# Split weights in seven named places, attention steps in another order, the experts' gate loaded behind the second rows

## The chip, the core and the metric

The kernel runs on one core of one Trainium2 chip. The metric is the device time of one execution in microseconds (us). PE is the matrix engine, PEld its weight loads, DVE the vector engine, ACT the scalar engine, POOL the GpSimd engine, SP the engine that here only issues transfers. L404 is line 404 of the kernel before. SBUF is the on-chip memory (tiles below are given per partition); PSUM holds matmul results in 8 banks of 128x512 fp32.

## What is computed (the reference, cut to what matters)

One layer of a diffusion backbone over 512 latent tokens and 256 context tokens, width 1024:

```python
h = ada_rmsnorm(x, g_mix, sh1, sc1); hc = ada_rmsnorm(ctx, ...)
proj = h @ w_in; proj_c = hc @ w_in[:, :CTX_COLS]
o_att = neighbourhood_attention(q, k, v, k_c, v_c, rpb)       # 8 heads of 64
x_l, x_c = short_conv(...), short_conv(...)                   # width 4
h_f, h_b = lru_direction(forward), lru_direction(backward)    # gated linear recurrences
o_lru = (h_f + h_b) * gelu(proj[..., LG])
y = sigmoid(ga) * (o_att @ w_up_attn) + sigmoid(gb) * (o_lru @ w_up_lru)
x = x + ga1 * (y @ w_out)
h2 = ada_rmsnorm(x, g_ffn, sh2, sc2)
x = x + ga2 * hier_moe(h2, ...)   # 32 experts, top 2 in the best group, SwiGLU
return rms(x) * g_final
```

All weights are fp32. The expert weights alone are 32 x 6 MB = 192 MB.

## The kernel before, in words

The order on each engine comes from a planner of the framework: the program is traced in order, and the planner puts each instruction into its engine's queue when its model says that it can run. `tc.high_priority()` moves instructions up, `tc.issue_after(i)` keeps an instruction behind `i` in its engine's queue; `queued()` (L69) does that along the chain `tail[0]`, so that PE's matmuls keep the traced order. A tile that is allocated again waits for the users of the place.

**Splitting weights.** The projections run at nearly fp32 accuracy as three fp32r products (`mm3`, L47: hi x hi, hi x lo, lo x hi). `wsplit` (L52) loads a raw weight tile by SP (L57), copies it to `hi` by ACT (L60, a cast) and subtracts on DVE (L61) to give `lo`. Raw and `lo` share a rotation of 4 places ("wlo"), `hi` has 3 ("whi"); later raw has a pool of its own with 2 places ("wraw"). A place has 4 KB, so it is 7 places and then 9. `next_weights` (L323) hands the weights out in a fixed order and traces the split of the weight after the one handed out.

**Stage 1 (to about 70 us):** modulation, norms, and the value projection `v_add` (L216), whose four weights also go through `wsplit`.

**Stage 2 (to about 465 us):** four rounds j of two heads each. `start` (L628) runs `keys`, `queries`, `lru_x(2j)`, then the first `scores(j, 0)`, then `lru_x(2j+1)`. `proj` (L334) is 8 x 3 matmuls of 512 columns for the latent part, in three pieces with a `yield` after each, and for keys and lru_x 24 of 256 columns for the context. `scores` (L391) writes two PSUM banks ("at"), one per head z; DVE adds the bias and finds the maximum (L411), ACT takes the exponential (L413), DVE the reciprocal (L414), ACT scales (L415): the result is P. `attend` (L421) goes over four blocks b: two steps of other work (`between`), `scores(b+1)`, then for each head four transposes of P into the single bank "pt" (L433), its copy to PT by DVE (head 0) or ACT (head 1) (L436), and one or two steps; then the product with the values (L444) and one step. The steps are `others(j)` (L638): gates, the LRU gates `lru_g` (L486), the LRU outputs `lru_o`, and in between `mod2` (L540), which loads the second part of the modulation weights on POOL's queue (L548) and sums them up on DVE (L552). The PSUM pool has at 2, pt 1, po 1, pj 4 banks. In `lru_g` a single tile "tr" holds the decay's gate of one direction, and the second direction's gate needs it again.

**Stage 3 (to about 530 us), "lift":** `lift` (L592) multiplies with the two up-projections in turn (weights `ua`, 12 matmuls, and `ul`, 24), DVE and ACT combine and split the result.

**Stage 4 (to 612 us):** output projection, router, top-2; POOL scatters token, weight and norm to DRAM tables `std` (L823); the first pair's rows are gathered by matmuls (L837).

**Stage 5 (from 612 us):** 16 pairs of experts. SP streams their weights, 12 transfers of 1 MB a pair ("w<-in_ew", L926), into 24 slots of 8 KB: `w0` to `w8` on the right side of SBUF, twelve `left` slots, and `we0` to `we2`. `wpool` (L888) says in which order they are used. `gu` (L1097) multiplies with the gate and up weights, 4 matmuls a chunk (L1102), `down` (L1107) with the down weights (L1115). For each later pair POOL gathers its token rows by an indirect transfer (`rows`, L950, L952), ACT scales them (L958), PE transposes (L962). `combine` (L1007) multiplies with the routing weight and with `ga2`, the residual's gate (L1012), and PE adds the result to the tokens (L1021, L1022). Before the first `rows`, POOL loads the eight `std` tables (L893), DVE sums them up (L894) and forms the token numbers `toki` (L900). The load of `ga2` (L1135, POOL, 512 KB by broadcast) goes into SBUF that the early slots `we1` and `we2` held, so it waits for the chunk with number 6:

```python
        rows(toki[:, 1:2])
        pgu[0] = [ps4.tile([128, 512], F32, name=f"g{v}") for v in range(2)]
        for pr in range(NE // 2):
            for k in range(1 if pr > 1 else 0, NK):
                if pr == 0 and k == EARLY[1] + 1:
                    wrx.close()
                    ...
                    G.dma_start(ga2, modd[3:4, :].to_broadcast([128, D]))
```

## Time and profile before

| | |
|---|---|
| median of 3 runs | 1086.6 us (1085.23 to 1088.78) |
| profiled execution, own time | 1088.48 us |
| its span, first to last instruction | 1086.7 us |
| mean granted TensorE clock | 0.978 |
| busy PE / DVE / ACT / POOL | 1003.9 / 558.2 / 430.1 / 95.9 us |
| moved by all DMA queues | 294.41 MB, 271 GB/s |

In the rows below, "PE pt L433 <- DVE PT L436: 14.4, 6, 3.7" reads: PE, at the instruction of line 433 that writes pt, waited for what DVE did in line 436, 14.4 us in total, 6 times, 3.7 us at the longest. In a timeline, [3.70 <-DVE PT L436] is the idle time of that engine before the row. A window's row has the busy time of each engine, the number of instructions, the granted clock (1.00 is 2.4 GHz, 0.50 is 1.2 GHz), the share of time in which the 16 DMA engines were busy, and GB/s.

### The profile page before, as it was taken

The numbers are of one execution on the slowest core, as the hardware profiler recorded it, in microseconds if no ns is written. First come the engines' busy times: TensorE is split into PE (matmuls) and PEld (weight loads), VectorE is DVE, ScalarE is ACT, GpSimd is POOL, SyncE is SP. The second block draws the span as 40 slices with busy tenths as digits, with TensorE's granted clock in tenths as the row PEclk, the third lists the DMA queues.
The fourth block names the chain that finished last, engine by engine and source line by source line (L and its number), as shares of the span: only waits on it lengthen the run. The fifth ranks groups of instructions, "written<-read, shape, count | busy, mean of one in ns | idle before, by whom it ended". The sixth has DMA issues, their size and how long they took to land. (4 is left out here: it accounts for less than half of the span.)

```text
span 1086.7 us, 13890 instructions
## 1 busy us (share of the span) xinstructions
PE 1003.9 (92%) x5226; PEld 619.7 (57%) x5226; DVE 558.2 (51%) x1146; ACT 430.1 (40%) x760; POOL 95.9 (9%) x160
## 2 busy tenths in 40 slices
PE   8999999897998998989999959999999999989895
PEld 7787667665776785768887523344444444333332
DVE  5678649576866566746557412333333353312224
ACT  4334873477267749823222112222222222212214
POOL 0021111011110001020100220000000000000001
PEclk9999999899999999999999979999999999999998
DMA  9585235244642222196597978999999999999992
GB/s 371 184 249 169 91 126 196 74 155 131 201 139 73 73 78 88 53 364 208 179 387 274 350 303 348 419 421 420 420 421 420 419 421 420 420 421 421 420 405 108
DMA packets 59176, 294.41 MB, mean 271 GB/s; under 512 B 8720, under 2 KB 9256, under 8 KB 33506
## 3 DMA queue, kind: packets, MB, share of 16 engines
q1 hardware_dynamic: 43634, 252.44, 58.8%
q0 software_dynamic: 12000, 34.75, 9.9%
q10 hardware_dynamic: 3472, 6.30, 1.5%
q8 instruction: 42, 0.69, 0.3%
q14 instruction: 28, 0.23, 0.1%
HBM read 287.76 MB, written 9.65 MB: 274 GB/s over the span
## 5 line engine op out<-in xcount | busy, mean ns | idle before, releaser
L1102 PE MATMUL g<-w,xg 128*64 128x512 f32 x1024 | 232.6, 598 | 5.9 <-DMA w<-in_ew 5.3
L1102 PEld LDWEIGHTS g<-w,xg 128*64 128x64 f32 x1024 | 68.2, 137 | 140.6 <-issue 119.6
L48 PE MATMUL pj<-hh,whi 128*128 128x512 f32 x320 | 132.7, 415 | 4.0 <-ACT gi L499 4.0
L49 PE MATMUL pj<-hl,whi 128*128 128x512 f32 x320 | 128.2, 401 | 0.0
L50 PE MATMUL pj<-hh,wlo 128*128 128x512 f32 x320 | 128.1, 400 | 0.0
L1115 PE MATMUL y<-w,hT 128*64 128x512 f32 x512 | 113.6, 593 | 4.3 <-DMA w<-in_ew 3.7
L965 ACT ACTIVATE xg<-pc,sh2col,s2col 128x128 f32<-128x128 f32 x120 | 45.1, 459 | 156.3 <-PE pc L962 156.3
L995 DVE TENSOR_TENSOR hm<-hm,g 128x512 f32<-128x512 f32 x16 | 11.0, 688 | 179.6 <-PE g L1102 166.4
L1024 DVE TENSOR_TENSOR x<-x,pc 128x512 f32<-128x512 f32 x122 | 75.8, 679 | 14.3 <-PE pc L1022 14.3
L1115 PEld LDWEIGHTS y<-w,hT 128*64 128x64 f32 x512 | 34.9, 137 | 79.4 <-issue 60.0
L61 DVE TENSOR_TENSOR wlo<-wlo,whi 128x1024 fp32r<-128x1024 f32 (+1 forms) x45 | 54.3, 1206 | 47.4 <-ACT whi L60 47.3
L48 PEld LDWEIGHTS pj<-hh,whi 128*128 128x128 f32 x320 | 61.2, 191 | 21.0 <-ACT gi L499 6.5
L1012 DVE SCALAR_TENSOR_TENSOR hm<-y,stok,ga 128x512 f32<-128x512 f32 x31 | 23.3, 751 | 95.4 <-PE y L1115 95.3
L1013 ACT CAST y_h<-hm 128x512 fp32r<-128x512 f32 x31 | 19.2, 619 | 133.3 <-DVE hm L1012 77.0
L50 PEld LDWEIGHTS pj<-hh,wlo 128*128 128x128 f32 x320 | 61.1, 191 | 15.0
L60 ACT CAST whi<-wlo 128x1024 fp32r<-128x1024 f32 (+1 forms) x45 | 46.6, 1035 | 56.5 <-DMA wlo<-in_wcol 37.3
L49 PEld LDWEIGHTS pj<-hl,whi 128*128 128x128 f32 x320 | 61.4, 192 | 12.3
L1021 PE MATMUL pc<-y_h,ot 128*128 128x512 f32 x122 | 52.2, 428 | 0.0
L1022 PE MATMUL pc<-y_l,ot 128*128 128x512 f32 x122 | 48.9, 401 | 0.0
L497 PE MATMUL pj<-xc,ga 128*128 128x256 f32 (+1 forms) x128 | 47.2, 510 | 1.5 <-ACT ga L533 1.3
L952 POOL DMA_INDIRECT xr<-nd,toki x15 | 16.7, 1112 | 347.4 <-PE pc L999 270.9
L552 DVE SCALAR_TENSOR_TENSOR acc<-m,c,acc 128x1024 f32<-128x1024 f32 x28 | 35.8, 1277 | 11.3 <-DMA m<-in_wm 11.3
(382 smaller groups left out, 1697.8 us busy)
## 6 DMA issues: line engine op xcount, KB each, us to landing
w<-in_ew SPq DMA_DIRECT2D x191, 1024.0 KB, 19.8
wlo<-in_wcol SPq DMA_DIRECT2D x40, 512.0 KB, 3.6
m<-in_wm POOLq DMA_DIRECT2D x32, 512.0 KB, 4.3
wm<-in_wm SPq DMA_DIRECT2D x8, 1024.0 KB, 10.1
bias<-in_rpb POOLq DMA_DIRECT2D x32, 128.0 KB, 2.5
gd<-ga ACTq DMA_DIRECT2D x16, 256.0 KB, 2.0
wraw<-in_ul SPq DMA_DIRECT2D x8, 512.0 KB, 3.8
woraw<-in_wout SPq DMA_DIRECT2D x16, 256.0 KB, 12.9
```

The source lines that it names most:

```text
L48: PE.matmul(o, wh, hh, start=start, stop=False)
L49: PE.matmul(o, wh, hl, start=False, stop=False)
L50: return PE.matmul(o, wl, hh, start=False, stop=stop)
L60: S.copy(hi[:, :n], raw[:, :n])
L61: V.tensor_tensor(lo[:, :n], raw[:, :n], hi[:, :n].bitcast(F32), op=ALU.subtract)
L497: m = PE.matmul(pg[:, 0:n], lw[:, 128 * w:128 * w + 128], xc[:, s0:s0 + n], start=True, stop=True)
L965: S.activation(xg[z][:, k % 4, :], pg[:, k % 4, :], AF.Identity, bias=sh2col[:, k:k + 1], scale=s2col[:, k:k + 1])
L1021: PE.matmul(pc, ot[:, i, :], y_h, start=True, stop=False)
L1022: m = PE.matmul(pc, ot[:, i, :], y_l, start=False, stop=True)
L1024: V.tensor_add(x2[:, i, ns], x2[:, i, ns], pc)
L1102: m = PE.matmul(pgu[pr][v][64 * e:64 * e + 64, :], xg[pr][k // 4][:, k % 4, 64 * e:64 * e + 64], w[:, v, e, :], start=(k == 0), stop=(k == ...
L1115: m = PE.matmul(py[64 * e:64 * e + 64, :], hT[:, k, 64 * e:64 * e + 64], w[:, k % 2, e, :], start=(k == 0), stop=(k == 3))
```

## The change

- `wsplit` takes its three places from `wplaces`: seven named tiles of 4 KB. The first four weights have written-out places; from then on raw rotates over three (2, 0, 1), `hi` over two (3, 5), `lo` over two (4, 6). The pool "wraw" is gone.
- `attend`: the transposes of both heads come first, into the shared "at" banks (now 3; "pt" is gone), then two steps, `scores(b+1)`, one step, the value product, one step. P has 2 places instead of 3.
- `lru_g`: the second direction's decay gate goes into half of `w2`; the decay of the first direction (ACT exponential, tanh, square, two DVE instructions) is traced after the second direction's first gate.
- `mod2_g`: two loading places, and places of their own for its two small tiles; two more yields.
- `start`: the first `scores` come after the latent part of `lru_x(2j+1)`.
- `wout` has two raw places instead of one (one more 2 KB), the unused "gap" pool grows from 18 to 24 KB, and the order of the left slots is adapted: three of them (9 to 11) lie in the gap, where two did before.
- the load of `ga2` is kept behind the first `rows` in POOL's queue.

```diff
--- before.py
+++ after.py
@@ -49,20 +49,30 @@
+    def wplaces():
+
+
+        yield from ((0, 1, 4), (3, 2, 5), (0, 3, 6), (0, 1, 4))
+        n = 0
+        while True:
+            yield (2, 0, 1)[n % 3], (3, 5)[n % 2], (4, 6)[n % 2]
+            n += 1
+
+    wplace = wplaces()
+
     def wsplit(src, shape):
-
         n = shape[0] * shape[1]
-        raw = (wraw[0] or ws).tile([128, 1024], F32, name="wraw" if wraw[0] else "wlo", bufs=2 if wraw[0] else 4)
+        r, h, l = next(wplace)
+        raw = ws.tile([128, 1024], F32, name=f"ws{r}")
         SP.dma_start(raw[:, :n], src)
-        lo = ws.tile([128, 1024], F32R, name="wlo", bufs=4)
-        hi = ws.tile([128, 1024], F32R, name="whi", bufs=3)
+        hi = ws.tile([128, 1024], F32R, name=f"ws{h}")
+        lo = ws.tile([128, 1024], F32R, name=f"ws{l}")
         S.copy(hi[:, :n], raw[:, :n])
...
-    wraw = [None]
     tail = [None]
@@ -391,7 +401,7 @@
         w0 = WIN[b]
-        scs = [ps.tile([128, 512], F32, name="at", bufs=2) for z in range(2)]
+        scs = [ps.tile([128, 512], F32, name="at", bufs=3) for z in range(2)]
         q = slice(128 * b, 128 * b + 128)
@@ -405,7 +415,7 @@
                 sc = scs[z]
-                P = p1.tile([128, 512], F32, name="P", bufs=3)
+                P = p1.tile([128, 512], F32, name="P", bufs=2)
                 st = p1.tile([128, 8], F32, name="st", bufs=4)
@@ -423,18 +433,19 @@
             between(2)
-            ahead_ = scores(j, b + 1, **kq) if b < 3 else None
             pts = []
-            for z in range(2):
-                with tc.high_priority():
-                    pt = ps.tile([128, 4, 128], F32, name="pt")
+            with tc.high_priority():
+                for z in range(2):
+                    pt = ps.tile([128, 512], F32, name="at", bufs=3).rearrange("p (k t) -> p k t", k=4)
                     with queued():
...
                     (S.copy if z else V.tensor_copy)(pts[z], pt)
-                between(1 + z)
+            between(2)
+            ahead_ = scores(j, b + 1, **kq) if b < 3 else None
+            between(1)
             with tc.high_priority():
@@ -484,26 +495,34 @@
         w2 = lp.tile([128, 2, 771], F32, name="w2")
-        for d in range(2):
-            cc = slice(8 * d + c, 8 * d + c + 1)
-            tr = lp.tile([128, 771], F32, name="tr")
-            for g, t in ((0, tr), (1, gi[:, d, :])):
-                w = 2 * d + g
-                bcol = (hba, hbx)[g][:, cc]
-                V.memset(t[:, 256:259], 0.0)
-                for (s0, n) in ((259, T), (0, TC)):
-                    pg = ps.tile([128, 512], F32, name="pj", bufs=4)
-                    with queued():
-                        m = PE.matmul(pg[:, 0:n], lw[:, 128 * w:128 * w + 128], xc[:, s0:s0 + n], start=True, stop=True)
-                    tail[0] = m.ins
-                    S.activation(t[:, s0:s0 + n], pg[:, 0:n], AF.Tanh, bias=bcol, scale=0.5)
-                if w < 3:
-                    yield
-            S.activation(a[:, d, :], tr, AF.Exp, bias=nsp4[:, cc], scale=nsp4[:, cc])
-            S.activation(tr, tr, AF.Tanh, bias=sp4[:, cc], scale=sp4[:, cc])
-            S.activation(w2[:, d, :], a[:, d, :], AF.Square)
-            V.scalar_tensor_tensor(w2[:, d, :], w2[:, d, :], 1.0, tr, op0=ALU.add, op1=ALU.mult)
+        cc = [slice(8 * d + c, 8 * d + c + 1) for d in range(2)]
+        tr = [lp.tile([128, 771], F32, name="tr"), w2[:, 1, :]]
+
+        def decay(d):
+
+            S.activation(a[:, d, :], tr[d], AF.Exp, bias=nsp4[:, cc[d]], scale=nsp4[:, cc[d]])
+            S.activation(tr[d], tr[d], AF.Tanh, bias=sp4[:, cc[d]], scale=sp4[:, cc[d]])
+            sq = lp.tile([128, 771], F32, name="tr") if d else w2[:, 0, :]
+            S.activation(sq, a[:, d, :], AF.Square)
+            V.scalar_tensor_tensor(w2[:, d, :], sq, 1.0, tr[d], op0=ALU.add, op1=ALU.mult)
             V.scalar_tensor_tensor(gi[:, d, :], gi[:, d, :], 1.0, xc, op0=ALU.add, op1=ALU.mult)
+
+        for w in range(4):
+            d, g = w // 2, w % 2
+            t = gi[:, d, :] if g else tr[d]
+            bcol = (hba, hbx)[g][:, cc[d]]
+            V.memset(t[:, 256:259], 0.0)
+            for (s0, n) in ((259, T), (0, TC)):
+                pg = ps.tile([128, 512], F32, name="pj", bufs=4)
+                with queued():
+                    m = PE.matmul(pg[:, 0:n], lw[:, 128 * w:128 * w + 128], xc[:, s0:s0 + n], start=True, stop=True)
+                tail[0] = m.ins
+                S.activation(t[:, s0:s0 + n], pg[:, 0:n], AF.Tanh, bias=bcol, scale=0.5)
+            if w == 2:
+                decay(0)
+            if w < 3:
+                yield
+        decay(1)
         S.activation(w2, w2, AF.Sqrt, scale=0.0625)
@@ -544,22 +563,22 @@
         for k in range(NK):
-            raw = m2.tile([128, 1024], F32, name="m2", bufs=2)
+            raw = m2.tile([128, 1024], F32, name=f"m{k % 2}")
             G.dma_start(raw, A["wm2"][g, k])
...
                 V.scalar_tensor_tensor(acc, raw, c32[:, k, 0:1], acc, op0=ALU.mult, op1=ALU.add)
-            if k < NK - 1:
-                yield
+            yield
         pm = ps.tile([128, 256], F32, name="pj", bufs=4)
...
             PE.matmul(pm[32 * j:32 * j + 32, :], ones[:, 0:32], acc[:, 256 * j:256 * j + 256], start=True, stop=True)
-        mr = m2.tile([128, 256], F32, name="m2", bufs=2)
-        mb = m2.tile([128, 256], F32, name="m2", bufs=2)
+        mr = m2.tile([128, 256], F32, name="mr")
+        mb = m2.tile([128, 256], F32, name="mb")
         V.memset(mb, 0.0)
...
         V.tensor_add(mr, pm, mb)
+        yield
         if g in (0, 3):
@@ -631,8 +650,11 @@
         run(lru_x(2 * j))
+        second = lru_x(2 * j + 1)
+        for _ in range(3):
+            next(second)
         Ps = scores(j, 0, **kq)
-        run(lru_x(2 * j + 1))
+        run(second)
         return kq, Ps
@@ -675,7 +697,6 @@
     yl = [yp.tile([128, NK, 128], F32R, name=f"yl{i}") for i in range(4)]
-    wraw[0] = l2.enter_context(pool("wraw"))
     tas = [lift(A["ua"][m], 4, 0, m) for m in range(2)]
@@ -691,7 +712,7 @@
             G.dma_start(wo["g", nh], modd[0:1, 512 * nh:512 * nh + 512].to_broadcast([128, 512]))
-        raw = pl.tile([128, 512], F32, name="woraw", bufs=bufs)
+        raw = pl.tile([128, 512], F32, name=f"woraw{k % bufs}")
         SP.dma_start(raw, A["wout"][nh, k])
@@ -701,7 +722,7 @@
             for k in (2 * m - 8, 2 * m - 7):
-                wout(0, k, wop, 1)
+                wout(0, k, wop, 2)
         ta = tas[m]
@@ -755,7 +776,7 @@
-    l2.enter_context(pool("gap")).tile([128, 18 * 256], F32, name="gap")
+    l2.enter_context(pool("gap")).tile([128, 24 * 256], F32, name="gap")
     with pool("p3") as p3, ExitStack() as xtx:
@@ -885,7 +906,7 @@
         left = [wx.enter_context(pool(f"w{i}")) for i in range(WR, WR + WL)]
-        wpool += [left[4], *left[10:12], left[0], left[2], *left[5:10], left[1], left[3]]
+        wpool += [*left[9:12], left[0], left[2], *left[4:9], left[1], left[3]]
         slot = chunks()
@@ -949,7 +970,7 @@
-            G.indirect_dma_start(xr, None, nd[:, :], bass.IndirectOffsetOnAxis(ap=tok, axis=0), bounds_check=T - 1,
+            return G.indirect_dma_start(xr, None, nd[:, :], bass.IndirectOffsetOnAxis(ap=tok, axis=0), bounds_check=T - 1,
                                  oob_is_err=False)
@@ -1123,7 +1144,7 @@
         pgu, dw = {}, [None]
-        rows(toki[:, 1:2])
+        rows1 = rows(toki[:, 1:2])
         pgu[0] = [ps4.tile([128, 512], F32, name=f"g{v}") for v in range(2)]
@@ -1132,7 +1153,8 @@
                     ga2 = p6.tile([128, D], F32, name="ga2")
-                    G.dma_start(ga2, modd[3:4, :].to_broadcast([128, D]))
+                    with tc.issue_after(rows1.ins):
+                        G.dma_start(ga2, modd[3:4, :].to_broadcast([128, D]))
                 gu(pr, k)
```

## Rows read from the trace of the kernel before

**Rows 1.** Busy time by windows: PE, PEld, DVE, ACT, POOL, clock, DMA share, GB/s.

```profile
80.00:460.00 380.00, 346.33 (x1881) 263.67 (x1881) 261.73 (x402) 246.00 (x376) 38.86 (x72) 0.98 0.37 119
644.00:658.00 14.00, 9.65 (x36) 5.61 (x38) 3.35 (x5) 5.82 (x11) 1.02 (x1) 0.65 0.26 77
658.00:1054.00 396.00, 387.05 (x1780) 153.26 (x1776) 128.62 (x220) 89.49 (x183) 14.75 (x14) 1.00 1.01 420
```

**Rows 2.** Waits of PE, 80 to 460 us: total us, times, longest us.

```profile
PE pt L433 <- DVE PT L436: 14.4, 6, 3.7
PE at L404 <- ACT qr L356: 6.7, 3, 5.1
PE pj L48 <- ACT gi L499: 4.0, 4, 1.6
PE pj L569 <- DVE m L562: 2.4, 1, 2.4
PE at L404 <- DVE qr L357: 2.1, 3, 0.8
PE pt L433 <- DVE st L414: 1.8, 3, 1.1
```

**Rows 3.** Timeline around block 2 of round 1, on PE, DVE and ACT.

```profile
240.68 0.66 PE L433 MATMUL pt<-ident,P 128*128 128x128 f32 x4
246.39 0.68 DVE L436 COPY PT<-pt 128x512 f32<-128x512 f32 x1
247.13 0.67 PE L433 MATMUL pt<-ident,P 128*128 128x128 f32 x4 [3.70 <-DVE PT L436]
247.18 1.34 ACT L415 ACTIVATE P<-P,st 128x512 f32<-128x512 f32 x2 [1.57 <-DVE st L414]
```

**Rows 4.** Timeline of PE behind the first scores of round 1.

```profile
195.97 0.63 PE L49 MATMUL pj<-hl,whi 128*128 128x512 f32 x1
196.40 0.63 PE L50 MATMUL pj<-hh,wlo 128*128 128x512 f32 x1
200.77 0.39 PE L50 MATMUL pj<-hh,wlo 128*128 128x512 f32 x1
201.01 0.40 PE L48 MATMUL pj<-hh,whi 128*128 128x512 f32 x1
```

**Rows 5.** Splits: idle before whi and wlo (us, times); a cast, a subtraction.

```profile
  DMA wlo<-in_wcol: 25.7, 11
232.25 1.05 ACT L60 CAST whi<-wlo 128x1024 fp32r<-128x1024 f32 x1
235.60 1.22 DVE L61 TENSOR_TENSOR wlo<-wlo,whi 128x1024 fp32r<-128x1024 f32 x1
```

**Rows 6.** Waits of PE, 460 to 660 us.

```profile
PE pj L50 <- DVE wlo L61: 3.1, 2, 1.7
PE pj L48 <- ACT whi L60: 2.1, 1, 2.1
```

**Rows 7.** Timeline at the start of stage 5, on POOL, DVE and PE.

```profile
612.83 1.17 POOL L893 DMA_DIRECT2D s<-std  x2
625.32 0.56 POOL L1135 DMA_DIRECT2D ga<-modd  x1 [10.37 <-issue]
625.86 3.20 POOL L893 DMA_DIRECT2D s<-std  x6
638.71 0.79 DVE L894 TENSOR_REDUCE stok<-s 128x48 f32<-128x384 f32 x1 [11.53 <-DMA s<-std]
629.51 7.09 PE L1115 MATMUL y<-w,hT 128*64 128x512 f32 x32 [0.67 <-ACT hT L1003]
642.23 1.06 POOL L952 DMA_INDIRECT xr<-nd,toki  x1 [13.17 <-DVE y_l L1014]
648.35 1.97 PE L962 MATMUL pc<-ident,xr 128*128 128x128 f32 x8 [11.76 <-ACT xr L958]
653.66 10.58 PE L1102 MATMUL g<-w,xg 128*64 128x512 f32 x48
```

## The prediction, made before the changed kernel ran

> **What bounds the kernel now.** I read the busy times by windows first [rows 1]. From 658 to 1054 us the DMA engines are busy all the time at 420 GB/s: the experts' weights arrive as fast as they ever do here. PE works 387.05 of these 396 us, on chunks that lie ready in 24 slots, and idles only where it has used them up. So the end is the end of the weight stream, plus 33 us of tail. Two things can move it: the moment at which stage 5 begins, which PE sets in stages 1 to 4 (346.33 busy of 380 us in stage 2), and holes in the stream once it runs. One hole is plain: from 644 to 658 us the DMA share is 0.26, so 14 x 0.74 = 10.4 us are lost, with all slots full and PE not consuming. A us taken from PE's idle time before 612 us, or from this hole, is a us at the end. Next I read PE's waits in stage 2 [rows 2], then the rows around single waits [rows 3, 4], the splitting of weights [rows 5], the lift [rows 6] and the start of stage 5 [rows 7].
>
> **a. Shared banks and the new order in attend.** PE's transposes waited 14.4 us in 6 waits for head 0's copy out of the only "pt" bank, and 1.8 us more that end with a DVE row of the same place [rows 2]. In [rows 3] head 0 is transposed at 240.68, DVE copies at 246.39, and head 1 has to wait until 247.13. With three banks head 1 needs no copy first. The copy must now be done when scores(b+1) wants the third bank, two steps later: a step is a third of a latent projection, 24 matmuls at 0.24 us [rows 4] = 5.8 us, so 1.9 us, and two are 3.9. The copy was 5.7 us behind, but with the bias work of scores ahead of it on DVE; that now stands behind it. What is late next is P. In [rows 3] the scores end where the transposes begin, at 240.68, and ACT's last scaling ends at 247.18 + 1.34 = 248.52: 7.8 us. Before, the order left some six steps and more for that; now four steps and the value product, about 7.7 + 1 us, so in an ordinary block 0.9 us is to spare, and in a block whose steps are the short ones of lru_g less. For block 0 there is only the context half of lru_x (256 of 512 columns, 2.9 us) and two steps, 6.8 us: 1 us late, four times. Bounds: 16.2 us gained, and 0 if P takes over everything. I take 10: 16.2 less 4 x 1.0 and 2.2 for the other twelve.
>
> The page TensorE: Matmul & The Clock Gate of the Trainium skill (section on HAM oscillation) speaks against this part: it tells of a kernel whose matmuls were put in a better order and says that "Adding PSUM double-buffering gave no further gain". By that this term is 0 and the sum below 19 instead of 29. The row of 14.4 us stands against it here.
>
> **b. First scores later.** PE waited 6.7 + 2.1 = 8.8 us for the rotated queries, once 5.1 us [rows 2]. Now 5.8 us of projection come first, more than the longest single wait. That work needs its own split weights in time: ACT stood 25.7 us in 11 waits for raw tiles [rows 5]. Three raw places let that load go out one weight earlier. Bounds 0 and 8.8; I take 6, nearer to the whole, since both halves of the cause are touched.
>
> **c. lru_g.** ACT, DVE and PE do the same number of instructions. The second direction's gate no longer waits for "tr", so its banks come free earlier; the wait for them is 4.0 us in 4 [rows 2]. The last gate's banks come free no earlier, as the first decay is now ahead of it on ACT. Bounds 0 to 4; taken 2.
>
> **d. mod2.** PE waited once, 2.4 us, for a small DVE sum that hangs on a load just issued [rows 2]. A yield now stands between. 8 more steps in all fit into the spare `next` calls. Taken 2 of 2.4. The loads themselves stay 32, on the same queue.
>
> **e. Clock.** After a long idle time PE runs at 1.2 GHz: matmuls start 0.43 us apart at 195.97, and 0.24 at 200.77 [rows 4]. In stage 2 the granted clock is 0.98 on average [rows 1], so 380 x 0.02 = 7.6 us are lost. If the waits halve, about half of the slow stretches go: 3.5. Bounds 0 and 7.6.
>
> **f. Seven places.** They add no instruction. Two prices. At the seam to stage 2 the first projection's `lo` takes the place of the value projection's last `lo`, so DVE can subtract only when PE is done with it: one subtraction, 1.2 us, partly behind two matmuls: +1. From then on `hi` and `lo` are two deep, where `hi` had three and `lo` shared four: the cast of weight n+2 cannot begin before PE has left weight n, and has the time of weight n+1. The rows show a cast at 232.25 whose subtraction, begun at 235.60, ends at 236.82 [rows 5]: 4.6 us with the queues' waits, against 5.8 us for a latent-only weight (4 queries, 16 gates, 8 lru_o: 28). It fits by 1.2 us. Bounds: 0, and 28 x 2 = 56 if the queues make 7.8 us of it, as they do for P. I take +4: four are late by 1 us.
>
> **g. Lift.** PE waited 3.1 + 2.1 us for split weights there [rows 6]. The raw pool of the lift lies where stage 2's tiles were; raw tiles in stage 2's own places can be loaded earlier. Against it: `ul` after `ua` has only 12 x 0.24 = 2.9 us for its split (cast 1.05, subtraction 1.2 at least), seven times, and one more early expert chunk (three gap slots, not two) shares the DMA. Bounds: 5.2 gained; 7 x (4.6 - 2.9) = 12 lost. Taken: 3 gained. The wout change and the other slot order cost nothing: DMA-bound stretches take the same bytes.
>
> **h. The gate behind the rows.** POOL issued the load of ga2 at 625.32, when its place came free, and only then six of the eight `std` loads, 625.86 to 629.06; they landed at 638.71, 9.65 us after the last. Then toki, the rows at 642.23, their scaling, and PE, idle for 11.76 us, transposed at 648.35, 6.1 us after the rows' issue [rows 7]. Freed of that, POOL issues the six loads from about 615 (after two of them at 612.83 and the memset) to 618.2; they land at 627.8; 3.5 us of sums and the queue later the rows go out, at 631.3. With 6.1 us to the transposes as before, or 4.7 more if the rows land as slowly as the tables did, PE can transpose from 637.4 to 642.1. It ends pair 0 at 629.51 + 7.09 = 636.6. The gate now goes out at 632.4 and lands at 642; combine waits for it: two steps on DVE and ACT, and PE adds from 643.5. Pair 1's first chunk is multiplied 1.9 to 3.7 us later (eight matmuls at either pace), 645.4 to 647.2 instead of 653.66 [rows 7]; the hole ends as much earlier [rows 1]. So 6.5 to 8.3 us of the hole close; I take 7.5. Bounds 0, if the gate lands as late as before, and the whole 10.4. The new wait is the one for ga2; behind it on POOL only the next pair's rows stand, which are needed in the middle of pair 1.
>
> **Sum.** 10 + 6 + 2 + 2 + 3.5 - 1 - 4 + 3 + 7.5 = 29 us. The profiled execution took 1088.48 us, with a span of 1086.7; less 29 it is 1059.5. It lies 1.9 us above the median of 1086.6, so the median to expect is 1057.6, rounded 1057.5.
>
> **Rivals.** 1. The waits only change their name: DVE and ACT are the late ones, P takes the place of the bank, and what PE gains at the scores it loses at the first transposes. For it: 7.8 us for P against 6.8 and 8.7 of cover. Against it: DVE is busy 261.73 and ACT 246.00 of 380 us [rows 1], neither is full. Then a, b, c and e give nothing: 1057.5 + 21.5 = 1079. What the Trainium skill says under a speaks for this rival, for term a alone. Half-way cases lie between. Chance 0.18.
>
> 2. Slower: the two-deep places. ACT's casts stand in one queue with everything else; if the cast and subtraction need 7.8 us from PE's release on average, each of the 28 latent-only weights makes PE wait 2 us: 56 instead of 4, so 1057.5 + 52 = 1109.5. It decides from 5.8 + 33/28 = 7.0 us on; below that the change is still faster. For it: ACT's casts already come late, 25.7 us of its idle time stand before them [rows 5]. Against it: that was for raw loads, which three places bring earlier, and the cast in the rows took 4.6. Chance 0.11.
>
> 3. All of the waits go, and the hole too: 16.2 + 8.8 + 4 + 2.4 + 7.6 + 5.2 + 10.4 = 54.6 less f's 1: 1033. A good part of that way, 1041, has a chance of 0.06.
>
> 4. The ordering of ga2 does nothing, since the `std` scatters land later than I think and the loads wait for those: h is 0, 1065. It is inside the forecast's own range.
>
> **How the numbers follow.** The forecast with its own range of 1043 to 1070 has 0.60; rival 1 0.18, rival 3 0.06, rival 2 0.11, and 0.05 that gains and losses of f and a cancel to within 0.3% (3.3 us, about what a measurement of this kernel can tell from no change). Faster by over 0.3%: 0.84. The range for 8 in 10 goes from 1041 to 1079: it takes in rival 1's time and most of rival 3's way, and leaves out rival 2, the tie and the far end.
>
> **What would show it.** PE's wait at the transposes for the copy should be gone and a wait for P of some us there instead (a); the wait at L404 for the queries under 3 us (b); waits of PE for whi and wlo in stage 2 of a few us, not tens (f); POOL's six `std` loads done by 620 us less what stage 2 gained, and PE's idle time before the first transposed rows short, followed by one for the gate (h); the DMA hole after pair 0 about 3 us; the stream then unbroken to its end. I am wrong if PE waits for split weights at every gate, or if stage 5 begins at 600 us or later.

## The result: 1056.2 us, and the profile after

The changed kernel takes 1056.17 us (median of 4 runs, 1054.95 to 1057.06), the kernel before 1087.69 in the same comparison: a ratio of 0.9703 [0.9664, 0.9742], or 31.5 us less. The forecast was 1057.5. The sum was right to 1.3 us; most of its terms were not, as the experiments show.

Against [rows 1] the windows of the changed kernel read (busy us of PE, PEld, DVE, ACT, POOL, then clock, DMA share and GB/s):

```profile
80.00:460.00 380.00, 365.27 (x1982) 280.78 (x1981) 274.42 (x418) 250.23 (x384) 43.80 (x83) 0.99 0.42 144
618.00:634.00 16.00, 15.36 (x62) 6.41 (x64) 4.89 (x7) 5.19 (x12) 0.00 (x0) 0.85 0.76 299
634.00:1022.00 388.00, 379.04 (x1744) 150.66 (x1741) 128.64 (x220) 89.26 (x183) 14.69 (x14) 1.00 1.01 420
```

The last stage is what it was: 420 GB/s, PE waiting only for chunks. The hole ahead of it has shrunk from 14 x 0.74 = 10.4 us to 16 x 0.24 = 3.8 us. From 80 to 460 us PE is busy 19 us more of the 380 (in the changed kernel this stretch holds stage 2 and the first 19 us of the lift). Stage 5 begins at 588.15 us instead of 612.43, 24.3 us earlier; the other 7.1 of the 31.4 by which the span shrank lie behind that.

The waits of PE in the same stretch as [rows 2] (total us, times, longest):

```profile
PE pj L48 <- ACT ws L71: 4.2, 1, 4.2
PE pj L48 <- ACT w L520: 3.3, 3, 1.1
PE pj L518 <- ACT gi L520: 3.0, 4, 1.5
PE pj L518 <- ACT tr L520: 1.6, 1, 1.6
PE pj L48 <- ACT gi L520: 1.1, 1, 1.1
PE pj L588 <- DVE mr L580: 0.8, 1, 0.8
PE pj L575 <- ACT w L520: 0.5, 1, 0.5
PE at L442 <- ACT P L425: 0.2, 1, 0.2
```

The wait for head 0's copy (14.4 us) is gone, and that for the rotated queries (8.8) too. P, which I had feared, costs 0.2. But the waits for banks that ACT empties at the gates (L520) are now 9.5 us in these rows where they were 4.8 (4.0 of them in [rows 2]), and the lift waits 4.2 us at once.

The start of stage 5 on POOL, DVE and PE, against [rows 7]:

```profile
590.56 3.23 POOL L914 DMA_DIRECT2D s<-std  x6
602.21 0.69 DVE L1016 TENSOR_TENSOR hm<-hm,g 128x512 f32<-128x512 f32 x1 [13.22 <-ACT hm L1015]
602.81 0.81 DVE L915 TENSOR_REDUCE stok<-s 128x48 f32<-128x384 f32 x1
605.81 1.06 POOL L973 DMA_INDIRECT xr<-nd,toki  x1 [12.03 <-DMA w<-in_ew]
606.88 0.57 POOL L1157 DMA_DIRECT2D ga<-modd  x1
617.18 0.75 DVE L1033 SCALAR_TENSOR_TENSOR hm<-y,stok,ga 128x512 f32<-128x512 f32 x1 [12.26 <-DMA ga<-modd]
614.13 1.10 PE L983 MATMUL pc<-ident,xr 128*128 128x128 f32 x8 [1.82 <-ACT xr L979]
618.64 0.79 PE L1042 MATMUL pc<-y_h,ot 128*128 128x512 f32 x1 [3.41 <-ACT y_h L1034]
622.65 10.52 PE L1123 MATMUL g<-w,xg 128*64 128x512 f32 x48
```

The six table loads no longer stand behind the gate; the last of them lands at 599.4. DVE sums them up only from 602.81 on, as a step of pair 0 that waits for ACT stands ahead in its queue. The token numbers are ready at 604.92, and the rows go out 0.9 us later, as in the kernel before (where the profile names DVE as the releaser). Counted from the start of stage 5, pair 1's first chunk is multiplied after 34.5 us instead of 41.2. The new wait is the one foretold: 3.4 us of PE for the product with the gate.

### The profile page after: what moved, and what is told of

Read it like the earlier page. It is cut to its first block, busy times and chain, and to the rows that moved or that the text cites. A ratio compares the mean times of both kernels' runs of the same rounds, so it can differ in the third digit from the quotient of the medians.

```text
span 1055.3 us, 13907 instructions
## 1 busy us (share of the span) xinstructions
PE 1000.6 (95%) x5226; PEld 618.2 (59%) x5226; DVE 561.5 (53%) x1146; ACT 428.1 (41%) x760; POOL 95.4 (9%) x160
## 4 chain that ended last, share of the span: by engine, by line
PE 75%; DMA 12%; ACT 7%; DVE 4%; issue 1%; ACTq 0%; SPq 0%; DVEq 0%; POOLq 0%
PE g L1123 17%; PE pj L48 10%; PE pj L49 9%; PE pj L50 9%; DMA w<-in_ew 9%; PE y L1136 8%; PE pc L1042 3%; PE pc L1043 2%; DMA ws<-in_ul 2%; PE po L798 1%; PE po L800 1%; PE po L799 1%; PE at L442 1%; PE pv L234 1%; PE pc L983 1%
## 5 line engine op out<-in xcount | busy, mean ns | idle before, releaser
L48 PE MATMUL pj<-hh,ws 128*128 128x512 f32 x320 | 129.7, 405 | 4.4 <-ACT w L520 3.3
L50 PE MATMUL pj<-hh,ws 128*128 128x512 f32 x320 | 126.4, 395 | 1.6 <-DVE ws L72 1.6
L49 PE MATMUL pj<-hl,ws 128*128 128x512 f32 x320 | 126.5, 395 | 0.0
L71 ACT CAST ws<-ws 128x1024 fp32r<-128x1024 f32 (+1 forms) x60 | 59.3, 989 | 73.9 <-PE pj L49 52.5
L72 DVE TENSOR_TENSOR ws<-ws,ws 128x1024 fp32r<-128x1024 f32 (+1 forms) x60 | 69.0, 1150 | 32.6 <-ACT ws L71 32.4
L48 PEld LDWEIGHTS pj<-hh,ws 128*128 128x128 f32 x320 | 60.1, 188 | 21.1 <-ACT w L520 5.3
L50 PEld LDWEIGHTS pj<-hh,ws 128*128 128x128 f32 x320 | 60.0, 188 | 16.6 <-DVE ws L72 2.0
L49 PEld LDWEIGHTS pj<-hl,ws 128*128 128x128 f32 x320 | 60.2, 188 | 12.4
L1042 PEld LDWEIGHTS pc<-y_h,ot 128*128 128x128 f32 x122 | 23.4, 192 | 32.7 <-issue 21.9
```

The lines of the kernel that those rows point to most:

```text
L48: PE.matmul(o, wh, hh, start=start, stop=False)
L49: PE.matmul(o, wh, hl, start=False, stop=False)
L50: return PE.matmul(o, wl, hh, start=False, stop=stop)
L71: S.copy(hi[:, :n], raw[:, :n])
L72: V.tensor_tensor(lo[:, :n], raw[:, :n], hi[:, :n].bitcast(F32), op=ALU.subtract)
L1042: PE.matmul(pc, ot[:, i, :], y_h, start=True, stop=False)
```

## The experiments

Twelve kernels. All medians, ratios and four marks of each profiled execution stand here first, so that a kernel can be looked up: the first matmul of the lift (the end of stage 2), of the output projection, of stage 5, and the span. "f", "d" and so on are the parts of the prediction.

| kernel | median us | ratio to before | lift | out. proj. | stage 5 | span |
|---|---|---|---|---|---|---|
| before | 1087.69 | | 466.6 | 539.9 | 612.4 | 1086.7 |
| after | 1056.17 | 0.9703 [0.9664, 0.9742] | 441.0 | 515.6 | 588.1 | 1055.3 |
| u_attend (after without a) | 1048.91 | 0.9662 [0.9638, 0.9686] | 438.6 | 510.3 | 581.2 | 1046.4 |
| u_scores (without b) | 1056.40 | 0.9719 [0.9693, 0.9744] | 440.5 | 517.7 | 588.3 | 1054.6 |
| u_lru (without c) | 1055.29 | 0.9710 [0.9685, 0.9735] | 439.6 | 516.5 | 589.0 | 1056.5 |
| u_gate (without h) | 1063.80 | 0.9794 [0.9771, 0.9818] | 440.0 | 516.3 | 587.1 | 1060.9 |
| u_places (without f) | 1059.30 | 0.9735 [0.9699, 0.9771] | 451.9 | 522.0 | 592.7 | 1061.6 |
| o_places (before with f) | 1082.37 | 0.9961 [0.9937, 0.9984] | 455.4 | 532.6 | 603.7 | 1078.6 |
| u_abc (before with f, d, h) | 1060.96 | 0.9788 [0.9765, 0.9811] | 445.0 | 522.0 | 592.9 | 1059.0 |
| u_ab (before with f, d, c, h) | 1048.88 | 0.9671 [0.9642, 0.9700] | 447.6 | 513.2 | 583.6 | 1047.5 |
| u_ac (before with f, d, b, h) | 1051.94 | 0.9690 [0.9670, 0.9711] | 436.8 | 514.9 | 585.7 | 1050.2 |
| pair | 1061.45 | 0.9762 [0.9728, 0.9796] | 444.0 | 522.1 | 594.7 | 1058.3 |
| late_chunks | 1056.18 | 0.9719 [0.9685, 0.9754] | 440.6 | 519.0 | 589.9 | 1053.9 |
| best2 | 1046.65 | 0.9631 [0.9613, 0.9650] | 438.7 | 510.0 | 580.7 | 1045.1 |

After, u_gate and late_chunks do the same work on PE up to the lift and reach it at 440.0 to 441.0, so there a mark is good to about 1 us. Each mark is that of a single execution: the profiled one of u_places is the slowest of its six, 4.0 us above their median, and that of u_lru 3.0 above, so their marks may be late.

### One part undone

**Attend** (u_attend):

```
-  scs: "at", bufs=3; P bufs=2; pt shares "at"; transposes, between(2), scores(b + 1), between(1)
+  scs: "at", bufs=2; P bufs=3; pt its own bank; scores(b + 1), transposes with between(1 + z)
-  mr, mb: places of their own
+  mr, mb in m0, m1 (so that the third P fits)
```

> The changed kernel with attend and scores as before: a bank of its own for the transposes, two score banks, three P places, scores(b+1) ahead of the transposes (so that it fits, two small tiles of mod2 share the places m0 and m1). Theory (part a is worth its waits and part of the clock): PE waits again for head 0's copy by DVE, about 16 us in stage 2, and the granted clock there falls from 1.00 to 0.98-0.99, so 4 to 8 us more: 1056 + 20 to 24 = 1076 to 1080 us, stage 5 begins 20 to 24 us later than at 588. Rival (the banks alone give nothing, the waits only move to another name): 1056 to 1060 us, stage 5 begins at 588 to 592 and the wait at the transposes is there, but another wait of the changed kernel is gone.

Measured: 1048.91 us, 7.3 **less**; its six runs (1047.78 to 1052.16) and the changed kernel's four do not overlap. Both the theory and its rival fell: the part costs time. (The edit also takes back the small tiles' own places, which was not tried by itself.) Undone, its old waits are back, but smaller than in [rows 2]:

```profile
PE pt L443 <- DVE PT L446: 7.4, 5, 2.3
PE pt L443 <- DVE st L424: 2.2, 2, 1.1
PE pj L517 <- ACT gi L519: 0.4, 2, 0.2
```

and the waits for gate banks are nearly gone. They are 9 us and more in every kernel with the new attend and 5 or less in every one without it, so in the changed kernel they are what attend's new order made of the old wait. It also slows the scores themselves. On PE's timeline, the twelve matmuls of one block in the changed kernel (the last line is the work behind them):

```profile
214.12 0.73 PE L414 MATMUL at<-kr,qr 64*128 64x256 f32 x4
214.58 0.28 PE L414 MATMUL at<-kx,qp 64*128 64x256 f32 x1
214.69 0.28 PE L414 MATMUL at<-kr,qr 64*128 64x256 f32 x1
214.70 0.28 PE L414 MATMUL at<-kx,qp 64*128 64x256 f32 x1
214.81 0.28 PE L414 MATMUL at<-kr,qr 64*128 64x256 f32 x1
214.82 0.62 PE L414 MATMUL at<-kx,qp 64*128 64x256 f32 x4
215.37 0.50 PE L48 MATMUL pj<-hh,ws 128*128 128x512 f32 x1
```

and with attend undone:

```profile
208.26 0.62 PE L414 MATMUL at<-kr,qr 64*128 64x256 f32 x6
208.72 0.52 PE L414 MATMUL at<-kx,qp 64*128 64x256 f32 x6
209.16 0.33 PE L443 MATMUL pt<-ident,P 128*128 128x128 f32 x1
```

1.25 us against 0.90. Eleven of the sixteen blocks take 1.25 us, one takes 1.13 and four 0.90; the 1.03 that the expectation of "pair" names below is in none. In the program the two heads alternate, one on the lower and one on the upper 64 rows of the array, and in the blocks of 0.90 us the twelve matmuls start two by two. In the block above three start alone, six two by two and three alone, as when one head is three matmuls ahead of the other. I take the reason to be that with three banks in one rotation head 1's bank comes free later than head 0's, so that the planner puts head 0's matmuls first; the order of the queue itself is not in the trace.

The scores lose 4.1 us by it (11 x 0.35 + 0.23). Against that, PE's waits in stage 2 are 1.8 us shorter with the new attend (10.5 against 12.3), and the clock gives 1.7. So without the slower scores the part would gain 3.5 us there; with them the sum is a loss of 0.6, where the mark says 2.3. The other 5 us of the 7.3 lie behind it, 3.0 of them in the lift (74.7 us against 71.7), and have no cause shown.

**First scores, lru_g and the gate, one at a time** (u_scores, u_lru, u_gate):

```
-  three steps of lru_x(2j+1), scores, the rest          (u_scores: scores ahead of lru_x(2j+1))
-  decay(0) behind the third gate, decay(1) at the end   (u_lru: each decay behind its two gates)
-  with tc.issue_after(rows1.ins): load of ga2           (u_gate: load of ga2 unordered)
```

> The changed kernel with the first scores ahead of the second lru_x, as before. Theory (part b): PE waits again for the rotated queries, 7 to 9 us over the four heads' starts, and 1 to 3 us of clock behind the longest of them: 1064 to 1068 us. Rival (the three raw places have already removed the cause, as the late split was what made the queries late): under 2 us of waits at the first scores, 1056 to 1058 us.

> The changed kernel with lru_g as before (one tr place, each direction's decay right behind its two gates). Theory (my sign for part c was wrong: with the first decay put between the third and the fourth gate's Tanh, the banks of these come free later): the 9.5 us of PE's waits for gate banks fall to about 4, the time to 1050 to 1052 us. Rival 1 (the rearrangement is needed, the wait for tr comes back on top): 9 to 14 us of waits, 1056 to 1062 us. Rival 2 (ACT is the engine that is behind here whatever the order): the waits stay within 2 us, 1054 to 1058 us.

> The changed kernel with the load of ga2 not ordered behind the second rows. Theory (part h): POOL holds six of the eight table loads behind ga2's place again, the rows and the first chunk of pair 1 come 7 us later, the DMA hole after pair 0 grows by 7 us: 1062 to 1065 us, stage 5 beginning at 588 as in the changed kernel. Rival (with the front shorter and the slots in another order the place of ga2 is free in time): below 1 us, 1055 to 1058 us.

Measured: 1056.40, 1055.29 and 1063.80. Undoing the first scores brings no wait for the queries back, as its rival said. Undoing lru_g leaves 9.0 us of gate-bank waits (4.5 + 3.3 + 1.2), so rival 2 held and, beside the new attend, lru_g's order was not their cause. The gate is worth 7.6 us, and POOL shows how:

```profile
600.04 0.56 POOL L1156 DMA_DIRECT2D ga<-modd  x1 [10.38 <-issue]
600.58 3.19 POOL L914 DMA_DIRECT2D s<-std  x6
616.33 1.06 POOL L973 DMA_INDIRECT xr<-nd,toki  x1 [12.55 <-DVE y_l L1035]
```

The second rows go out 29.2 us after stage 5 begins, as before (29.8), where the changed kernel has 17.7.

**The places** (u_places) and **the places alone** (o_places):

```
-  r, h, l = next(wplace); raw, hi, lo in ws0 ... ws6
+  raw and lo from one ring of four, hi from a ring of three; the lift's raw pool; gap 18; slots as before
   (o_places: the kernel before with the first of these and not the second)
```

> The changed kernel with the split weights in the places of before (raw and lo in one ring of four, hi in a ring of three, the lift's own raw pool, the gap and slot order of before). Theory (the seven places carry the front gain, since undoing the first scores and lru_g changed nothing and undoing attend made it faster): the waits for the rotated queries come back through late splits, the clock falls below 1.00, 1056 + 14 to 24 = 1070 to 1080 us. Rival 1 (the forecast's term, the places cost 4 + 1 and give 3 at the lift): 1052 to 1058 us. Rival 2 (each part alone is enough to hide the same waits): 1056 to 1060 us.

> The kernel before with the seven places alone (and the gap, the slot order and the output weights' two names that go with them); attend, first scores, lru_g, mod2 and the gate as before. Theory (the places carry the front gain): 1087 - 14 to 22 = 1065 to 1073 us, the waits for the queries, 8.8 us, under 2, stage 2's clock 0.99 or more, ACT's idle time for raw tiles gone. Rival (the places only help with the other parts): 1080 to 1088 us.

Undone, 1059.30; alone, 1082.37: both near the rivals, small effects on the time (alone 4.8 us below 1087.15, the runs of before beside them, a ratio of 0.9961 [0.9937, 0.9984]; undone 3.1 us, with runs that overlap those of the changed kernel). The marks say more. At the end of stage 2 the places are worth 11.2 us alone (466.6 to 455.4) and up to 10.9 when taken from the changed kernel (451.9 against 441.0, from the slowest run of u_places); the lift hands 4 of it back, 73.3 us long before, 77.2 with the places alone. What they do in stage 2 is in ACT's waits from 68 to 440 us. The changed kernel without them:

```profile
ACT whi L60 <- DMA wlo<-in_wcol: 46.6, 17, 4.9
```

The places alone in the kernel before:

```profile
ACT ws L71 <- DMA ws<-in_wcol: 4.1, 1, 4.1
```

The changed kernel, where no such row is left and the casts wait for PE to leave a place:

```profile
ACT ws L71 <- PE pj L49: 34.6, 24, 3.1
```

A cast that waits for its raw load holds ACT, and the subtraction behind it holds DVE. That had also made some of the copies late. The timeline of ACT and DVE in the kernel before, ahead of the copy at 141.60, with PE idle for 2.12 us behind it:

```profile
137.52 1.05 ACT L60 CAST whi<-wlo 128x1024 fp32r<-128x1024 f32 x1 [2.26 <-DMA wlo<-in_wcol]
138.60 1.23 DVE L61 TENSOR_TENSOR wlo<-wlo,whi 128x1024 fp32r<-128x1024 f32 x1 [2.20 <-ACT whi L60]
```

The copy stands behind both, and so does that of 350.33 (a wait of 2.14); with the places alone these two waits are gone. In the block of [rows 3] the same chain held DVE for 0.37 us only: the subtraction, the bias work of scores, a sum of mod2 and a gate fill the 5.1 us from the transposes to the copy, and with the places alone 2.76 of its 3.70 us stay. The copy of 262.39 (a wait of 2.95) was late for another reason, a load of mod2, on DVE:

```profile
259.44 1.28 DVE L552 SCALAR_TENSOR_TENSOR acc<-m,c,acc 128x1024 f32<-128x1024 f32 x1 [4.52 <-DMA m<-in_wm]
```

With the places alone, the two rows of waits at the transposes come to 6.3 us instead of 16.2, the bank being the same. And the casts' new wait costs PE nothing in stage 2: the two-deep price that I had set at 4 did not come.

### Scores in turn, and the lift's loads

**pair**: the twelve score matmuls of a block chained to each other.

```
+  with tc.issue_after(m.ins) if m else nullcontext():
       m = PE.matmul(scs[z][:, cs], ...)
```

> The changed kernel with the twelve score matmuls of a block chained to each other, so that both heads' stay in turn; nothing else. In the changed kernel's queue twelve of the sixteen blocks have head 0's six ahead of head 1's six, and such a block takes 1.03 to 1.25 us from its first start to the next work's start, where the kernel with attend undone takes 0.90. Theory (matmuls on the two halves of the array overlap only when they stand in turn): 12 x 0.13 to 0.35 us, 2 to 4 us less, 1052 to 1054 us, scores' busy time (both rows together) from 26 to 18 us. Rival (the bank for head 1 comes free late, so the group as a whole starts later and PE waits there instead): 1056 to 1060 us, a wait of PE for PT at the scores.

Each block is back at 0.90 us (214.38 to 215.28), and the kernel is 5.3 us slower: stage 2 ends 3 us later, the gate-bank waits go to

```profile
PE pj L520 <- ACT gi L522: 7.8, 8, 2.8
```

and the clock to 0.98 from 180 to 360 us. Neither range was met (1061.45 us is above the rival's 1060), and PE does not wait for PT at the scores, as the rival had it; why the gate-bank waits grow instead was not traced further. So the pace is real, but mending it alone does not pay.

**late_chunks**: the four early expert chunks behind one of the lift's raw loads.

```
-  with tc.issue_after(loaded[0]) if n in late[4:] else nullcontext():
+  with tc.issue_after(loaded[0]) if n in late[4:] else tc.issue_after(raws[-7]):
```

> The changed kernel with the four expert chunks that go out at 435 to 441 us ordered behind the lift's fourth latent weight on SP. Theory (their 4 MB delay the lift's raw weights by some 9 us, DMA share 1.02 in 440:460): the lift's waits, 6.0 us, fall under 2 and the clock from 0.88 to near 1.00 there, 1056 - 5 to 8 = 1048 to 1051 us. Rival (the chunks then delay the later raw weights or the output weights instead, or the wait is ACT's own queue): 1054 to 1058 us.

Nothing (1056.18). The chunks had stood ahead of the lift's weights; on SP, in the changed kernel:

```profile
435.76 2.41 SPq L947 DMA_DIRECT2D w<-in_ew  x3
438.35 0.82 SPq L716 DMA_DIRECT2D woraw<-in_wout  x2
439.55 0.33 SPq L68 DMA_DIRECT2D ws<-in_ua  x1
```

with the cast of that ua at 455.56, 16 us after the issue. But with the chunks gone the output weights moved into their place, and their casts into ACT's queue ahead of the lift's. On ACT and PE in late_chunks:

```profile
449.64 0.62 ACT L719 CAST wo<-woraw 128x512 fp32r<-128x512 f32 x1 [4.30 <-DMA woraw<-in_wout]
451.26 0.79 PE L48 MATMUL pj<-hch,ws 128*128 128x512 f32 x1 [5.08 <-ACT ws L72]
```

### Two and three parts undone: what took the front's time

Attend undone, and with it the first scores (u_ab), lru_g (u_ac), or both (u_abc); the edits are those above.

> The changed kernel with attend and the first scores as before. Theory (with the raw places and mod2's own steps the queries are in time whatever the order; undoing the first scores alone changed nothing): within 2 us of attend undone alone, 1047 to 1051 us, no wait at the first scores. Rival (attend's new order had been hiding the queries' wait, so b and a covered for each other): 6 to 9 us of waits for the queries and some clock, 1055 to 1061 us.

> The changed kernel with attend and lru_g as before. Theory (the gate-bank waits of the changed kernel, 9.5 us, are the price of attend's new order and not of lru_g; with attend undone 1.7 us are left whichever lru_g): 1048 to 1051 us. Rival (lru_g's new order is what removed them, 4 us of waits and the clock behind them come back): 1053 to 1058 us.

> The changed kernel with attend, first scores and lru_g all as before: what is left of the change is the seven places, mod2's two added yields and the gate behind the rows. Theory (undoing the first scores or lru_g beside attend cost 0 and 3 us, so mod2's yields and the places hold the front gain together): 1049 to 1054 us, waits for queries and gate banks under 6 us in all. Rival (the first scores and lru_g's order can each stand in for the other, both out brings their waits of 6.5 and 4.3 us and some 7 us of clock back): 1060 to 1070 us; the places alone had 1082.4, and the gate is worth 7.6, so 1074.8 would mean that mod2's yields give nothing.

Measured 1048.88, 1051.94 and 1060.96. The first two stay near attend undone alone by their times, but u_ab's end of stage 2 is 9.0 us later (447.6 against 438.6), with the waits for the queries back at 5.2 us, as its rival said; the lift hid that, with no wait of PE and 65.6 us. u_ac lies between its theory and its rival, and u_abc met the rival's range. It is 23.7 us below its own runs of before (1084.67); the places alone had 4.8 and the gate has 7.6, so 11.3 are left for mod2's yields, much more than the 2 I gave them. The transposes of mod2 on the timeline, without the yields (o_places):

```profile
261.93 0.44 PE L579 MATMUL pj<-ident,m 128*128 128x128 f32 x2 [3.12 <-DVE m L572]
```

and the window there:

```profile
260.00:270.00 10.00, 8.07 (x32) 6.57 (x33) 7.40 (x11) 1.97 (x3) 1.61 (x3) 0.83 0.55 191
```

With them (u_abc):

```profile
243.35 0.44 PE L579 MATMUL pj<-ident,m 128*128 128x128 f32 x2 [0.29 <-ACT gi L509]
```

Without the yield the sum stands behind lru_g's scans on DVE and PE idles 3.1 us, and the granted clock is 0.83 in the 10 us around that. The clock also falls behind waits of other kinds in o_places (2.8 us for the copy, 2.6 and 2.1 for the queries, and once 1.0), so that it is 0.94 from 180 to 270 and 0.96 from 270 to 360 us (9.0 us); u_abc has 0.98 and 1.00 (1.8 us). How much of the 10.4 us at the mark is the yields' own and how much is waits that fall better by chance stays open: the wait itself is one of 3.1 us. (In u_abc the small tiles lie in the two loading places, as before, so they are not the cause.)

### A faster kernel

**best2**: attend undone, and three edits: the seam's places swapped, the gate behind the last table load, and the chunks and output weights behind the lift's raw loads.

```
-  yield (2, 0, 1)[n % 3], (3, 5)[n % 2], (4, 6)[n % 2]
+  yield (2, 0, 1)[n % 3], (5, 3)[n % 2], (6, 4)[n % 2]
-  with tc.issue_after(rows1.ins): load of ga2
+  with tc.issue_after(tab8.ins): load of ga2
+  with tc.issue_after(raws[-1]) if nh == 0 else nullcontext(): load of woraw
+  the expert chunks as in late_chunks
```

> The kernel with attend undone (1048.9 us) and three edits: the seam's places swapped (hi in places 5 and 3, lo in 6 and 4, so the first projection's lo does not take the value projection's last), the gate of the combination behind the last table load rather than behind the second rows, and at the lift the four early expert chunks and the output weights' first loads ordered behind the lift's raw loads. Theory: the seam's wait of 1.6 us goes, the hole after pair 0 closes by up to 3.9, the lift's waits of 3.2 + 0.5 and the lost clock there (0.07 x 20 + 0.01 x 40 us) go: 1049 - 7 to 11 = 1038 to 1042 us. Rival at the lift (moving the chunks alone changed nothing; the DMA engines were then held by 2 MB of x and the output weights, and ACT's casts stood behind these): no gain there, 1042 to 1045 us. Rival at the gate (the rows now stand behind the gate on POOL and come as much later): hole as before, 3.9 us more than the theory.

Measured 1046.65 us, ratio 0.9631 [0.9613, 0.9650]: the lowest median here, 2.3 us below attend undone, where I had expected 7 to 11 less; the intervals of the two ratios overlap. The seam keeps 1.4 of 1.6 us. The gate closes nothing of the hole: PE's wait of 2.8 us for the gated product becomes one of 2.5 for the rows. At the lift the theory held for as long as nothing stood ahead: PE is busy 20.00 of 20 us from 440 to 460 (16.27 with attend undone alone). Then, on SP,

```profile
460.89 1.95 SPq L948 DMA_DIRECT2D w<-in_ew  x4
462.94 1.17 SPq L69 DMA_DIRECT2D ws<-in_ul  x1
```

and on ACT and PE

```profile
478.62 1.04 ACT L72 CAST ws<-ws 128x1024 fp32r<-128x1024 f32 x1 [2.02 <-DMA ws<-in_ul]
479.72 0.50 PE L48 MATMUL pj<-hch,ws 128*128 128x512 f32 x1 [2.79 <-ACT ws L72]
```

the next raw weight comes 15.7 us after its issue, behind 4 MB. Ordering the chunks behind the last raw weight was not tried.

## Why the prediction was right, and which of its steps were wrong

The sum of 29 was met by 31.4 because wrong terms cancelled, which is luck; h alone came as priced. For stage 2 the terms can be read off the table by adding the parts one by one to the kernel before, at the mark of the lift: f takes 466.6 to 455.4, d to 445.0 (u_abc), b to 436.8 (u_ac), c back up to 438.6 (u_attend), a to 441.0 (after). Each step is one execution against one other, and another order would give other steps.

- **a, forecast +10: wrong in sign.** It costs 2.3 us in stage 2, and 7.3 in all by the medians. The failed step is "the copy was 5.7 us behind" as a price of the bank: the copy was behind late splits, a late load of mod2 and other work of DVE, and f alone, with the bank as it was, removed 9.9 of the 16.2 us. What I had as rival 1 happened to this part, not with P but with gate banks and with heads out of turn. The section on HAM oscillation of TensorE: Matmul & The Clock Gate in the Trainium skill, which I had set aside, said that double-buffering gave nothing further there; here the part with the third bank did not pay either, though the 14.4 us of waits were real. Without b, a does gain in stage 2 (447.6 to 440.5): the two hide the same waits, and I had added them. By the medians it loses there too (1048.88 to 1056.40), for the lift grows by 11.6 us.
- **b, forecast +6:** 8.2 to 9.0 in stage 2 with attend as before, nothing beside the new attend. By the medians it is 9.0 (u_abc to u_ac) and nothing (u_ab to u_attend).
- **c, forecast +2: wrong in sign in stage 2,** where it loses 1.3 to 2.7 us in each of the three pairs (u_lru, u_ac, and u_ab against u_abc). The wait that I priced does go: with attend as before, the gate banks cost 4.9 us without c (u_ac) and 0.7 with it (u_attend). What I left out is that another wait comes in its place. In u_ac, to be set against the rows of u_attend above:

```profile
PE pj L48 <- ACT gi L509: 2.7, 3, 1.5
PE pt L443 <- DVE PT L446: 2.6, 3, 1.3
```

  The wait for the copy is 2.6 us there and 7.4 with c (1.9 and 6.5 in the other pair); why DVE's copy is later was not traced. By the medians c does not lose: 0.9 us, within the noise, beside the new attend, and a gain of 3.0 and 12.1 us with attend as before, where the lift is 6.4 and 11.4 us shorter with it.
- **d, forecast +2:** 10.4 with the clock, the largest miss in size.
- **e, forecast +3.5:** stage 2's clock went from 0.98 to 1.00 between 80 and 440 us, nearly all of the 7.6. It does not come with f: with the places alone the clock is still 0.98 there; in the steps above it is inside d and b.
- **f, forecast -5 (seam 1, two-deep 4): wrong in sign,** +11.2 in stage 2. The seam cost 1.6. The two-deep price of 4 measured 0 in stage 2: the casts wait 34.6 us for PE to leave a place, and PE never waits for a cast. The term left out what the new places give, the end of ACT's waits for raw loads; rows 5 showed them (25.7 us), and I used them only for b. By the medians f gives less, 4.8 us alone and 3.1 in the changed kernel.
- **g, forecast +3: wrong in sign.** From the first lift matmul to the output projection it takes 74.7 us against 73.3, and 65.6 to 78.5 over all kernels with these places (70.2 in u_places). The failed step is that the raw tiles come earlier: a raw weight behind the chunks is ready only 16 us after its issue. I had named one more early chunk and not priced it; but late_chunks, with all four moved, still takes 78.5, so that the chunk is the cause is not shown. The other failed step is that the second raw place of the output weights, part of the same edit, was put at nothing: in the changed kernel ACT's cast of an output weight waits 6.85 us for its load (until 451.57), ahead of the lift's cast at 455.56 that PE waits for. How much of the lift's length is owed to which stays open.
- **h, forecast +7.5:** 7.6 by the medians, and nearly step by step as worked out: rows 17.7 us after stage 5 began (18.9 forecast), transposes 26.0 (25.0 to 29.7), pair 1 at 34.5 (33.0 to 34.8). Two misses inside cancelled: the tables landed after 11.3 us instead of 15.4, and DVE's queue then held their sum for 3.4.

## What to carry to other kernels

When several waits on one engine are to go, price the cause they share before the symptoms: here a late load held an in-order cast, which held an in-order subtraction, which held a copy in two of six waits, and three parts of the change each claimed the same microseconds. Undo parts one at a time and in pairs, and read them at a mark inside the kernel, for a later stage can hide or hand back what an earlier one gained. A right sum is no evidence for its terms: this change holds a part that costs 7.3 us, and without it the kernel takes 1048.9 us.

## What the runs showed of the hardware

- **Matmuls of 64 rows on the two halves of the array overlap best when they start two by two:** twelve take 0.90 us then, 1.13 with one half two ahead of the other and 1.25 with one half three ahead. The Trainium skill, TensorE: Matmul & The Clock Gate, Part 3 on packing, says that a weight load overlaps a running matmul only on other rows; the rows here do not agree, for loads of all 128 rows run beside matmuls of all 128 rows. Matmuls of 512 columns start 0.23 us apart in the changed kernel, and each load takes 0.19 us. This one is for the matmul that starts at 440.49, while the one before it starts at 440.26:

```profile
440.26 0.19 PEld L49 LDWEIGHTS pj<-hl,ws 128*128 128x128 f32 x1
```

- **A short idle time can cost nearly as much again, but need not.** In u_attend PE idled 2.25 us ahead of 320.75, and the granted clock from 320 to 325 us was 0.66, between the levels of 1.2 and 2.4 GHz: matmuls then start 0.43 us apart instead of 0.23, and 5 x 0.34 = 1.7 us are lost. In the kernel before, an idle time of 2.95 us ahead of 263.13 was followed by no drop. In u_places the clock fell to 0.68 between 215 and 220 us, where PE had only waits of 0.7, 0.9 and 1.1 us close together. In the changed kernel, whose longest single wait from 80 to 440 us was 1.63 us, it was 1.00 throughout. The windows in u_attend and in the kernel before:

```profile
320.00:325.00 5.00, 4.25 (x12) 3.27 (x13) 2.61 (x6) 2.92 (x5) 1.60 (x3) 0.66 0.61 195
260.00:270.00 10.00, 7.05 (x44) 5.42 (x44) 6.12 (x9) 8.26 (x10) 0.00 (x0) 1.00 0.01 2
```

- **A 512 KB load issued 2 us behind four of 1 MB is ready 15.7 us later** (best2), where the median of the 40 loads of that size in stage 2 lands after 3.7.
